# Seven products in place of eight for most of the first layer's input projection, with q, k, v and z parked in DRAM and the attention moved beside the conv output product

## The chip, the cores and the metric

The kernel runs on one core of one Trainium2 chip. The metric is device time in microseconds (us) of one execution; lower is better. TensorE (PE in the profile) does the matrix products, VectorE (DVE) and ScalarE (ACT) the element-wise work, GpSimd (POOL) some of it together with a DMA queue of its own, and SyncE (SP) issues most transfers.

## The reference

Two blocks follow each other on an activation of 1024 tokens by 1024 channels; the change lies in the first. All tensors are f32.

```python
h = rms_norm(x, norm_g)
u = h @ w_in        # v_c b_c c_c z_c q(1024) k(256) v(256) z_a gate_logits(2048)
y_c = b_c * causal_depthwise_conv(c_c * v_c, conv_w)
y_c = y_c * silu(z_c)
y_a = y_c @ w_conv_out
q = rms_norm(q per head, q_norm_g); k = rms_norm(k per head, k_norm_g)
o = sliding_window_attention(q, k, v, sinks) * silu(z_a)
y_b = o @ w_attn_out
gates = sigmoid(gate_logits + gate_b); g_a, g_b = split(gates, 2)
x = x + (g_a * y_a + g_b * y_b) @ w_out
```

The attention has 16 query heads and 4 key heads of 64 channels, blocks of 128 tokens and a window of 128. The second block (pooling and gated linear attention, cross attention, a feed-forward part) is not touched.

## The kernel before

**Layout.** Activations lie transposed, 128 channels by 512 tokens a tile; `kt` counts the eight channel tiles and `h` the two halves of the tokens. Every f32 operand is split into a high part and a low part (`S.copy` on ACT makes the high one, a subtraction on DVE the low one), and a product is three matmuls: high by high, high by low, low by high. A page is the weights for 128 output channels; it is loaded from DRAM on SP's queue into one of two raw buffers, cast on ACT (L282) and subtracted on DVE (L346).

**A dense step.** `dense(w, act, h)` is 24 matmuls of 512 columns into one PSUM bank. It calls `tick()` in its middle, and its caller calls `tick()` again behind it. A tick moves every generator in the list `side` one step on; that is how other work is set between matmuls. All engines take their instructions in the order in which the program writes them (`manual_schedule`).

**Seven products.** `wino` does two pages by two token halves as a 2 by 2 block product with seven half-size products in place of eight: 84 matmuls in place of 96. It needs sums of weight blocks (four additions on POOL for each page pair, L299 to L307, with their splits on ACT and DVE) and sums of activation blocks, T1 to T4, which the generator `sums` makes once for one norm (16 subtractions and 16 splits, started by `hT_sums`, which first reads the normalised activations back from DRAM). Each result is handed out in the middle of the sequence, through one of four callbacks: `c11` (as it lies in PSUM), `c22` and `c12` (a DVE addition or subtraction of a saved product makes them first) and `c21` (as it lies). Behind each callback stands a `tick()`.

```python
        prod(x, "A12", "B21", False)
        c11(x)
        tick()
        prod(y, "S3", "T3", False)
        c22(y, q5)
        tick()
```

**Order of the first block before the change.** k and v; z, eight pages, dense; q, eight pages, dense, each loaded twice because the order is by token half; the first four gate pages `gb`; the other gates and the attention output pages `ao`; the conv pages `cc`, `cv`, `cz`, `cb` for eight channel tiles, tile 0 dense and 1 to 7 by seven products; the gates `ga` by seven products; the conv output `co`, dense; then the output projection `wo`.

**The attention** is a generator of 32 units (two key pairs `p`, two halves `h`, four token blocks `b`, two head halves). Each step of it, one to a tick, takes the units through a pipeline: `scores` (PE, then DVE and ACT; for the first token block POOL first fills the tile, L892), `expo` (ACT), `finish` (POOL, L929), `turn` (PE transposes, then two POOL selections, L959), `differ` (POOL, L937 to L943, every second step) and `values` (PE, L972). It runs beside q and the first four gate pages. For each q tile, `stats` squares the tile on ACT (L846), sums over channels with eight small matmuls (L855) and takes a power on POOL (L859); `q_group` calls it one tick after the square is issued, in the middle of the next dense step.

Of the kernel before, what the change touches and what calls it, by code (L numbers as in the profile page):

```python
# [14 lines left out]
P = 128  # L15
# [63 lines left out]
def _stream():  # L79
    st = [("v", 0), ("v", 1)]  # L80
    st += [("z", p, j) for p in range(2) for j in range(4)]
    st += [("q", p, j) for p in range(2) for h in range(2) for j in range(4)]
    st += [("gb", m) for m in range(4)] + [("ao", m) for m in range(4)]
    for m in range(4, KT):
        st += [("gb", m), ("ao", m)]
    for c in range(KT):
        names = [("cc", c), ("cv", c), ("cz", c), ("cb", c)]
        st += names if c == 0 else [("pair", names[0], names[1]), ("pair", names[2], names[3])]
    st += [("pair", ("ga", m), ("ga", m + 1)) for m in range(0, KT, 2)]
    st += [("co", m) for m in range(KT)]  # L90
# [27 lines left out]
def _body(es, tc, nc, wp, vec, xT, memT, gk2, pw, cst, out, dbg):  # L118
# [39 lines left out]
    def dram(s):  # L158
        n = nm(s)
        return dpool.tile([P, HT], F32, name=n, tag=n)  # L160
# [546 lines left out]
    kp = [(pg("kh", F32R), pg("kl", F32R)) for _ in range(2)]  # L707
    wk = [[], []]
# [23 lines left out]
    def k_evac(o, p, h):  # L732
# [6 lines left out]
        def thread():  # L739
# [27 lines left out]
            V.tensor_tensor(kl[:, sl], kg, f(kh[:, sl]), ALU.subtract)  # L767

# [48 lines left out]


    oT = [[[None, None] for _ in range(4)] for _ in range(2)]

    def z_evac(p, j):
        def run(o, h):
            t = hp("o")
            S.activation(t, o, AF.Silu)
            oT[p][j][h] = t
        return run

    for p in range(2):
        for j in range(4):
            if (p, j) == (0, 0):  # L830
                first_two(("z", 0, 0), ("z", 0, 1), hT, z_evac(0, 0), z_evac(0, 1))
            elif (p, j) != (0, 1):
                both(("z", p, j), hT, z_evac(p, j))

    qT = {}
    rqt = {}

    def q_group(p, h):
        rq = spool.tile([P, 4, 4, 2], F32, name=nm("rq"), tag="rq", bufs=3)
        rqt[p, h] = rq  # L840
        for j in range(4):
            w = W.get(("q", p, j), pf=False)
            o = dense(w, hT, h, mid=W.pf)
            tick()
            sq = tp("qsq")
            S.activation(sq, o, AF.Square)  # L846
            qh, ql = hp("qh", F32R), hp("ql", F32R)
            S.activation(qh, o, AF.Copy, scale=col("q_norm_g"))
            V.scalar_tensor_tensor(ql, o, col("q_norm_g"), f(qh), ALU.mult, ALU.subtract)
            qT[p, j, h] = (qh, ql)  # L850

            def stats(sq=sq, j=j):
                st = ps("t", (P, 4, 64))
                for t in range(4):
                    T.matmul(st[:, t, :], sq[:, t * P:(t + 1) * P], blk2.rearrange("p a b -> p (a b)"), start=True, stop=True)  # L855
                ms = sm("ms", (P, 8))

                V.tensor_scalar(ms.rearrange("p (a b) -> p a b", b=2), st[:, :, 0:64:32], 1.0, 64 * EPS, ALU.mult, ALU.add)
                G.tensor_tensor(rq[:, :, j, :], ms.rearrange("p (a b) -> p a b", b=2),  # L859
                                mhalf.rearrange("p (a b) -> p a b", b=2), ALU.pow)  # L860
                return
                yield

            side.append(stats())
# [115 lines left out]
    def attention():  # L980
        units = [Unit(p, h, b, half) for p in range(2) for h in range(2) for b in range(4) for half in range(2)]
        n = len(units)
        todo = [(j, h) for j in range(4) for h in range(2)]
        dv = None
        yield
        for i in range(n + 3):
            if 0 <= i - 1 < n:
                units[i - 1].expo()
            if 0 <= i - 3 < n:
                units[i - 3].values(dv)  # L990
            if i % 2 == 0 and 0 <= i - 2 < n and units[i - 2].n:
# [7 lines left out]
            if i >= n - 6 and todo:  # L999
                j, h = todo.pop(0)  # L1000
                osp[j][h] = split(oT[0][j][h], "o")
            yield
        while todo:
            j, h = todo.pop(0)
            osp[j][h] = split(oT[0][j][h], "o")
        for h in range(2):
            for j in range(4):
                osp[4 + j][h] = split(oT[1][j][h], "o", tp if j == 3 else None)
                if j % 2:
                    yield  # L1010

    q_group(0, 0)
    side.append(attention())
    for p, h in ((0, 1), (1, 0), (1, 1)):
        q_group(p, h)
    mg = []

    def gb_evac(m, fn):
        t = pg("mg")
        mg.append(t)  # L1020

        def run(o, h):
            S.activation(t[:, h * HT:(h + 1) * HT], o, fn, bias=col("gate_b", 8 + m))
        return run

    for m in range(4):
        both(("gb", m), hT, gb_evac(m, AF.Identity if m < 3 else AF.Sigmoid))
    drain()
    for m in range(3):
        S.activation(mg[m], mg[m], AF.Sigmoid)  # L1030

    mgd = grid(KT)

    def ao_evac(m):
        def run(o, h):
            sl = slice(h * HT, (h + 1) * HT)
            V.tensor_tensor(mg[m][:, sl], mg[m][:, sl], o, ALU.mult)
            mgd[m][h] = dram("mgd")
            nc.sync.dma_start(mgd[m][h], mg[m][:, sl])
        return run  # L1040

    for m in range(4):
        both(("ao", m), osp, ao_evac(m))
    for m in range(4, KT):
        both(("gb", m), hT, gb_evac(m, AF.Sigmoid))
        both(("ao", m), osp, ao_evac(m))
    dump("mgb", mg[0])


    reopen("q1pool", 16)  # L1050
    XB = {}

    def hT_sums():
        t = {}
        order = [(kt, h) for k in range(4) for kt, h in ((k, 0), (k, 1), (k + 4, 1))] + [(k, 0) for k in range(4, 8)]

        def loads():
            for i, (kt, h) in enumerate(order):
                t[kt, h] = (hp if (kt < 4) == (h == 0) or kt == 7 else hq)("ht")
                nc.sync.dma_start(t[kt, h], hraw[kt, h])  # L1060
                if i in (3, 7, 9, 11, 13):
                    yield

        g = loads()
        for _ in range(3):
            next(g)
            yield
        side.append(g)
        yield from sums(t, XB, {"T1": hp, "T2": hp, "T3": hq, "T4": hq})

    yc, ycd = grid(KT), grid(KT)

    class Conv:


        def __init__(self, c):
            self.c, self.cs, self.accs, self.cv = c, [None, None], [None, None], [None, None]

        def cc(self, o, h):
            self.cs[h] = tp("cc")  # L1080
            S.copy(self.cs[h], o)

        def cv_tile(self, h):
            self.cv[h] = tp("cvp", shape=(P, HT + 2))
            if h == 0:
                G.memset(self.cv[h][:, 0:2], 0.0)
            return self.cv[h][:, 2:]

        def taps(self, h):
            w0, w1, w2 = (col("conv_w", k * 8 + self.c) for k in range(3))  # L1090
            cv = self.cv[h]
            if h:
                V.tensor_copy(cv[:, 0:2], self.cv[0][:, HT:HT + 2])
            acc = self.accs[h] = tp("yc")
            V.tensor_scalar(acc, cv[:, 0:HT], w0, None, ALU.mult)
            V.scalar_tensor_tensor(acc, cv[:, 1:HT + 1], w1, acc, ALU.mult, ALU.add)
            V.scalar_tensor_tensor(acc, cv[:, 2:HT + 2], w2, acc, ALU.mult, ALU.add)

        def cv_evac(self, o, h):
            V.tensor_tensor(self.cv_tile(h), o, self.cs[h], ALU.mult)  # L1100
            self.taps(h)

        def cz(self, o, h):
            t = tp("csz")
            S.activation(t, o, AF.Silu)
            V.tensor_tensor(self.accs[h], self.accs[h], t, ALU.mult)

        def cb(self, o, h):
            V.tensor_tensor(self.accs[h], self.accs[h], o, ALU.mult)
            ycd[self.c][h] = dram("ycd")  # L1110
            nc.sync.dma_start(ycd[self.c][h], self.accs[h])

        def first(self):
            def c22(y, q5):
                V.tensor_tensor(self.cv_tile(1), y, q5, ALU.add)

            def c12(z, q5):
                t = self.cs[1] = tp("cc")
# [3 lines left out]
            def c21(y):  # L1122
                self.cv_evac(y, 0)
                self.taps(1)
# [910 lines left out]
```

## Time and profile before

| | |
|---|---|
| Median of three runs | 2454.65 us (2453.22 to 2457.58) |
| The profiled execution's own time | 2452.95 us |
| Its span, from the first to the last instruction | 2451.2 us |
| PE busy | 2406.3 us, 98% |
| DVE, ACT, POOL busy | 1408.7, 964.5, 519.1 us |
| Mean granted TensorE clock | 0.996 |
| DMA | 223.00 MB, mean 91 GB/s |

A busy time adds up the instructions that overlap nothing; matmuls are pipelined, so that one of 512 columns is shown as 0.39 us long while the next one starts 0.23 us after it. Lengths of stretches are therefore taken from start to start.

### The profile page before, as it was taken

How to read it: one execution, taken by the hardware profiler on the slowest of the kernel's cores; microseconds unless marked ns; L12 is line 12 of the kernel's file. 1: busy time of each engine (PE TensorE's matmuls, PEld its weight loads, DVE VectorE, ACT ScalarE, POOL GpSimd, SP SyncE). 2: the span in 40 equal slices, each digit the busy share in tenths (PEclk: the TensorE clock that was granted, in tenths of full speed). 3: DMA queues.
4: the chain of work that ended last, by engine and by line, in shares of the span. 5: the costliest groups of instructions: out<-in, count | busy, mean ns of one | idle time of the engine just before them, and what ended most of it. 6: DMA issues, size and time to landing. Idle time of an engine off the chain costs nothing.

```text
span 2451.2 us, 30538 instructions
## 1 busy us (share of the span) xinstructions
PE 2406.3 (98%) x11694; PEld 1973.6 (81%) x11694; DVE 1408.7 (57%) x2223; ACT 964.5 (39%) x1784; POOL 519.1 (21%) x529
## 2 busy tenths in 40 slices
PE   8999999999999999999999999999999999999998
PEld 7887777888888888886888888888778887878887
DVE  6416676118666634555435556555678888874435
ACT  5326665113333242234322334444455555552212
POOL 3115653003333321021001110001223333310003
PEclk9999999999999999999999999999999999999999
DMA  4211111223222138231110245222422222244222
GB/s 156 92 53 52 35 40 41 84 85 122 69 73 74 61 109 304 87 97 51 35 36 29 79 128 180 95 82 95 155 78 82 78 78 78 78 150 158 90 80 91
DMA packets 86259, 223.00 MB, mean 91 GB/s; under 512 B 9792, under 2 KB 12256, under 8 KB 86112
## 3 DMA queue, kind: packets, MB, share of 16 engines
q1 hardware_dynamic: 82992, 212.65, 25.6%
q0 software_dynamic: 2576, 7.87, 0.9%
q8 instruction: 92, 1.51, 0.2%
q10 hardware_dynamic: 544, 0.52, 0.1%
q14 instruction: 55, 0.45, 0.1%
HBM read 180.11 MB, written 40.89 MB: 90 GB/s over the span
## 4 chain that ended last, share of the span: by engine, by line
PE 82%; DVE 8%; ACT 5%; POOL 2%; issue 2%; DMA 1%; SPq 0%; DVEq 0%; POOLq 0%; ACTq 0%
PE psmm L382 16%; PE psmm L384 16%; PE psmm L383 16%; PE pss L411 4%; PE pss L412 4%; PE pss L413 4%; PE psmm L412 3%; PE psmm L411 3%; PE psmm L413 3%; ACT pr L921 1%; PE pst L413 1%; PE pst L412 1%; PE pst L411 1%; PE pso L412 1%; PE pso L411 1%
## 5 line engine op out<-in xcount | busy, mean ns | idle before, releaser
L382 PE MATMUL psmm<-xnh,wh 128*128 128x512 f32 x832 | 332.8, 400 | 3.0 <-ACT wh L282 3.0
L384 PE MATMUL psmm<-xnh,wl 128*128 128x512 f32 x832 | 326.5, 392 | 2.6 <-DVE wl L346 2.6
L383 PE MATMUL psmm<-xnl,wh 128*128 128x512 f32 x832 | 325.6, 391 | 1.1 <-POOL u L1730 0.8
L346 DVE TENSOR_TENSOR wl<-wr,wh 128x1024 fp32r<-128x1024 f32 (+2 forms) x163 | 196.6, 1206 | 210.4 <-ACT wh L282 210.2
L282 ACT CAST wh<-wr 128x1024 fp32r<-128x1024 f32 (+2 forms) x163 | 165.1, 1013 | 272.7 <-PE psmm L383 264.3
L567 POOL TENSOR_TENSOR sq<-sq,sq 128x512 f32<-128x512 f32 (+1 forms) x58 | 70.6, 1217 | 643.8 <-ACT sq L563 642.8
L299 POOL TENSOR_TENSOR ws<-wr 128x512 f32<-128x512 f32 x37 | 57.8, 1563 | 634.1 <-DMA wr<-in_wp_dram 557.2
L382 PEld LDWEIGHTS psmm<-xnh,wh 128*128 128x128 f32 x832 | 157.0, 189 | 42.4 <-issue 5.8
L384 PEld LDWEIGHTS psmm<-xnh,wl 128*128 128x128 f32 x832 | 156.9, 189 | 38.0 <-DVE wl L346 4.3
L383 PEld LDWEIGHTS psmm<-xnl,wh 128*128 128x128 f32 x832 | 157.0, 189 | 33.6 <-POOL u L1730 1.2
L411 PE MATMUL pss<-T,wsh 128*128 128x512 f32 x444 | 176.9, 398 | 0.4
L413 PE MATMUL pss<-T,wsl 128*128 128x512 f32 x444 | 174.4, 393 | 0.0
L412 PE MATMUL pss<-T,wsh 128*128 128x512 f32 x444 | 174.4, 393 | 0.0
L331 DVE TENSOR_TENSOR wsl<-ws,wsh 128x512 fp32r<-128x512 f32 x148 | 145.3, 1024 | 18.2 <-ACT wsh L313 18.2
L384 PE MATMUL psmm<-fh,wl 128*128 128x512 f32 (+1 forms) x300 | 116.0, 387 | 1.0 <-DVE wl L346 1.0
L413 PE MATMUL psmm<-xnh,wl 128*128 128x512 f32 x296 | 115.4, 390 | 0.8 <-DVE wl L303 0.8
L382 PE MATMUL psmm<-fh,wh 128*128 128x512 f32 (+1 forms) x300 | 116.0, 387 | 0.0
L383 PE MATMUL psmm<-fl,wh 128*128 128x512 f32 (+1 forms) x300 | 115.9, 386 | 0.0
L412 PE MATMUL psmm<-xnl,wh 128*128 128x512 f32 x296 | 115.5, 390 | 0.0
L411 PE MATMUL psmm<-xnh,wh 128*128 128x512 f32 x296 | 115.4, 390 | 0.0
L563 ACT ACTIVATE sq<-x 128x512 f32<-128x512 f32 (+1 forms) x80 | 47.1, 588 | 165.3 <-DVE x L1250 110.0
L1741 DVE SCALAR_TENSOR_TENSOR fa<-u,vt,fa 128x512 f32<-128x512 f32 x88 | 79.2, 900 | 48.8 <-ACT fa L1740 45.1
(442 smaller groups left out, 5832.4 us busy)
## 6 DMA issues: line engine op xcount, KB each, us to landing
wr<-in_wp_dram SPq DMA_DIRECT2D x230, 512.0 KB, 3.5
act<-fa SPq DMA_DIRECT2D x44, 256.0 KB, 2.1
fr<-act SPq DMA_DIRECT2D x44, 256.0 KB, 4.6
wr<-in_wp_dram SPq DMA_DIRECT2D x24, 384.0 KB, 3.1
xd<-x SPq DMA_DIRECT2D x32, 256.0 KB, 4.4
x<-xd SPq DMA_DIRECT2D x32, 256.0 KB, 3.9
x<-in_xT_dram SPq DMA_DIRECT2D x16, 256.0 KB, 5.3
hraw<-xn SPq DMA_DIRECT2D x16, 256.0 KB, 2.0
```

What stands on the lines that cost most here:

```text
L282: S.copy(hi[:, :n], raw[:, :n])
L299: G.tensor_tensor(sg[0], a21, a22, ALU.add)
L331: V.tensor_tensor(lo, raw, f(hi), ALU.subtract)
L346: V.tensor_tensor(lo, raw, f(hi), ALU.subtract)
L382: T.matmul(out_ap, lh, rh, start=first, stop=False)
L383: T.matmul(out_ap, lh, rl, start=False, stop=False)
L384: T.matmul(out_ap, ll, rh, start=False, stop=last)
L411: T.matmul(o, lh, rh, start=first and kt == 0, stop=False, skip_group_check=True)
L412: T.matmul(o, lh, rl, start=False, stop=False, skip_group_check=True)
L413: T.matmul(o, ll, rh, start=False, stop=kt == 3, skip_group_check=True)
L567: eng.tensor_tensor(self.acc, self.acc, sq, ALU.add)
L1741: V.scalar_tensor_tensor(a, u[:, 1:HT + 1], w1, a, ALU.mult, ALU.add)
```

## The change

- z of `p` 1, all of q, all of `gb` and the conv tile 0 go by seven products, twelve page pairs more. `hT_sums` starts in the z stage, as soon as the second half of the norm is done and k and v are on their way to DRAM.
- k, v, q (both parts each), z and both gates are written to DRAM on SP's queue as they are made.
- The attention starts with `co`. `att_in` reads k, q, v and z back on POOL's queue: for both `p` of half 0 ahead of `co` (16 and 14 transfers of 256 KB), and for half 1 at the attention's steps 9 and 17 (16 and 14). Its units are ordered by half first.
- `co` and `ao` run by token half, so each of their pages is loaded and split twice; q's pages only once. The product of `co` with its gate goes to DRAM and comes back in `ao`, which now ends the stage.
- `stats` of q is put in `side` inside the callback, so it runs at the tick right behind it.

The core of the diff:

```diff
 def _stream():
     st = [("v", 0), ("v", 1)]
-    st += [("z", p, j) for p in range(2) for j in range(4)]
-    st += [("q", p, j) for p in range(2) for h in range(2) for j in range(4)]
-    st += [("gb", m) for m in range(4)] + [("ao", m) for m in range(4)]
...
+    st += [("z", 0, j) for j in range(4)]
+    st += [("pair", ("z", 1, j), ("z", 1, j + 1)) for j in (0, 2)]
+    st += [("pair", ("q", p, j), ("q", p, j + 1)) for p in range(2) for j in (0, 2)]
+    st += [("pair", ("gb", m), ("gb", m + 1)) for m in range(0, KT, 2)]
     for c in range(KT):
...
+        st += [("pair", ("cc", c), ("cv", c)), ("pair", ("cz", c), ("cb", c))]
     st += [("pair", ("ga", m), ("ga", m + 1)) for m in range(0, KT, 2)]
-    st += [("co", m) for m in range(KT)]
+    st += [("co", m) for m in range(KT)] * 2
+    st += [("ao", m) for m in range(KT)] * 2
...
+    def hT_sums():
+        while None in [x[1] for x in hT] or len(kd) < 8 or len(vd) < 4:
+            yield
+        reopen("q1pool", 16)
...
+    def q_out(p, j, h, o):
...
+        sq = tp("qsq")
+        S.activation(sq, o, AF.Square)
+        qh, ql = tp("qh", F32R), tp("ql", F32R)
+        S.activation(qh, o, AF.Copy, scale=col("q_norm_g"))
+        V.scalar_tensor_tensor(ql, o, col("q_norm_g"), f(qh), ALU.mult, ALU.subtract)
+        qd[p, j, h] = dram("qdh"), dram("qdl")
+
+        def stats():
+            for dst, src in zip(qd[p, j, h], (qh, ql)):
+                nc.sync.dma_start(dst, f(src))
+            st = ps("t", (P, 4, 64))
+            for t in range(4):
+                T.matmul(st[:, t, :], sq[:, t * P:(t + 1) * P], blk2.rearrange("p a b -> p (a b)"), start=True, stop=True)
...
+        side.append(stats())
...
+    def pair(na, nb, X, evac):
+
+        def c22(y, q5):
+            t = tp("c22")
+            V.tensor_tensor(t, y, q5, ALU.add)
+            evac(1, 1, t)
...
+        wino((na, nb), X, lambda x: evac(0, 0, x), c22, c12, lambda y: evac(1, 0, y))
...
+    while "T1" not in XB:
+        tick()
...
+    for j in (0, 2):
+        pair(("z", 1, j), ("z", 1, j + 1), XB, lambda i, h, o: z_out(1, j + i, h, o))
+    for p in range(2):
+        for j in (0, 2):
+            pair(("q", p, j), ("q", p, j + 1), XB, lambda i, h, o: q_out(p, j + i, h, o))
...
+    reopen("gpool2", 8)
...
+    def att_in(p, h):
+
+        if h == 0:
+            kp[p] = pg("kh", F32R), pg("kl", F32R)
+        for i in range(2):
+            nc.gpsimd.dma_start(f(kp[p][i][:, h * HT:(h + 1) * HT]), kd[p, h, i])
         for j in range(4):
...
+            qT[p, j, h] = hp("qh", F32R), hp("ql", F32R)
+            for i in range(2):
+                nc.gpsimd.dma_start(f(qT[p, j, h][i]), qd[p, j, h][i])
...
+        units = [Unit(p, h, b, half) for h in range(2) for p in range(2) for b in range(4) for half in range(2)]
...
+            if i in (9, 17):
+                att_in(i // 16, 1)
...
+    for p in range(2):
+        att_in(p, 0)
+    gate_in(gin, gad, 0, 0)
     while None in [yc[c][0] for c in range(KT)]:
         tick()
...
+    side.append(attention())
+    for h in range(2):
+        for m in range(KT):
+            w = W.get(("co", m))
+            gate_in(gin, gad, m + 1, h)
+            if h == 0 and m == 4:
+                side.append(reload([(ycd[c][1], yc[c], 1) for c in range(KT)], "yc", 2))
...
+            o = dense(w, yc, h)
+            t = gin[m, h]
+            V.tensor_tensor(t, t, o, ALU.mult)
+            mcd[m][h] = dram("mcd")
+            nc.sync.dma_start(mcd[m][h], t)
+            tick()
```

## Rows read from the trace of the kernel before

**Rows 1.** The page: busy time of each engine (share of the span) and its instructions.
```profile
PE 2406.3 (98%) x11694; PEld 1973.6 (81%) x11694; DVE 1408.7 (57%) x2223; ACT 964.5 (39%) x1784; POOL 519.1 (21%) x529
```

**Rows 2.** Timeline of PE, conv tile 0: start, us, instruction, count, idle before.
```profile
545.17 0.40 PE L382 MATMUL psmm<-xnh,wh 128*128 128x512 f32 x1
...
588.71 0.62 PE L445 MATMUL pss<-xnh 128*128 128x512 f32 x2
```

**Rows 3.** Timeline of PE, first matmuls of the second and the eighteenth seven-product pair.
```profile
609.47 0.39 PE L411 MATMUL psmm<-xnh,wh 128*128 128x512 f32 x1
...
918.22 0.39 PE L411 MATMUL psmm<-xnh,wh 128*128 128x512 f32 x1
```

**Rows 4.** Timeline of PE: first matmul of `values`, units 1, 22 and 28.
```profile
204.64 0.39 PE L972 MATMUL pso<-pch,vh 128*128 128x512 f32 x1
...
345.26 0.39 PE L972 MATMUL pso<-pch,vh 128*128 128x512 f32 x1
...
379.77 0.40 PE L972 MATMUL pso<-pch,vh 128*128 128x512 f32 x1
```

**Rows 5.** Timeline of PE: a group of `stats` between two matmuls of a dense step.
```profile
168.66 1.00 PE L855 MATMUL pst<-blk,qsq 128*128 128x64 f32 x8
169.47 0.48 PE L382 MATMUL psmm<-xnh,wh 128*128 128x512 f32 x1
```

**Rows 6.** POOL's power by line, and what L972 waited for.
```profile
L859 POOL TENSOR_TENSOR rq<-ms,mhalf x16: 1650/2553/2557, 169.9 to 346.1; 128x8 f32<-128x8 f32 x16
...
  POOL pph L959: 12.5, 21
```

**Rows 7.** Timeline, the kernel's end: addition, square, sum over channels [idle before <- releaser].
```profile
2441.01 0.42 DVE L1890 TENSOR_TENSOR x<-x,psmm 128x256 f32<-128x256 f32 x1 [1.02 <-PE psmm L384]
2441.53 0.42 ACT L563 ACTIVATE sq<-x 128x256 f32<-128x256 f32 x1 [1.08 <-DVE x L1890]
2442.00 0.55 PE L574 MATMUL pst<-mC,sq 128*128 128x64 f32 x3 [0.18 <-ACT sq L563]
```

**Rows 8.** Timeline, seven products: the last matmul of a product, its reader on ACT.
```profile
591.88 0.39 PE L413 MATMUL psmm<-xnh,wl 128*128 128x512 f32 x1
...
592.31 0.58 ACT L418 ACTIVATE pss<-psmm 128x512 f32<-128x512 f32 x1 [2.47 <-PE psmm L413]
```

**Rows 9.** By line, ns shortest/median/longest: square of q, addition as in `c22`, splits of T.
```profile
L846 ACT ACTIVATE qsq<-psmm x16: 597/610/622, 166.1 to 337.4; 128x512 f32<-128x512 f32 x16
...
L1772 DVE TENSOR_TENSOR u<-pss,q x19: 691/692/693, 1837.5 to 2189.5; 128x512 f32<-128x512 f32 x19
...
L462 DVE TENSOR_TENSOR T<-ht,T x16: 677/685/1781, 570.6 to 603.1; 128x512 fp32r<-128x512 f32 x16
```

**Rows 10.** Timeline of POOL as `co` begins: first and last transfers of 24.
```profile
936.52 0.54 POOL L1212 DMA_DIRECT2D mg<-mgd  x1 [18.81 <-PE pss L413]
...
950.21 3.17 POOL L645 DMA_DIRECT2D x<-in_xT_dram  x5 [0.20 <-issue]
```

**Rows 11.** Windows: busy of PE, PEld, DVE, ACT, POOL; clock, DMA share, GB/s.
```profile
936.50:954.00 17.50, 17.50 (x78) 14.45 (x77) 10.35 (x17) 6.86 (x13) 12.25 (x23) 1.00 0.96 350
...
339.00:414.00 75.00, 74.12 (x412) 59.11 (x411) 55.88 (x157) 49.06 (x150) 36.02 (x55) 1.00 0.09 29
```

**Rows 12.** By line, L904 on DVE: idle time until the fill on POOL (us, times).
```profile
  POOL pr L892: 5.8, 3
```

**Rows 13.** Timeline, attention beside `gb`: last selection of a pair, its reader on PE.
```profile
368.67 0.63 POOL L959 TENSOR_SCALAR_AFFINE_SELECT ppl<-pcl 128x512 fp32r<-128x512 f32 x1
...
380.47 0.39 PE L972 MATMUL pso<-pph,dvh 128*128 128x512 f32 x1
```

**Rows 14.** Windows round two pauses of PE, with the granted clock behind each.
```profile
20.90:25.40 4.50, 0.97 (x8) 0.77 (x8) 4.36 (x6) 3.28 (x6) 1.21 (x1) 1.00 0.61 243
25.50:28.90 3.40, 3.40 (x19) 3.40 (x18) 1.93 (x4) 0.00 (x0) 0.00 (x0) 0.50 0.02 5
76.00:87.00 11.00, 8.77 (x43) 7.14 (x42) 7.43 (x13) 7.03 (x10) 5.85 (x5) 1.00 0.40 143
```

More of the change, by code (lines that the diff above doesn't have):

```diff
@@ L835, in _body @@
[L835 to L840, printed above, removed]
-        for j in range(4):
[L842 to L864, printed above, removed]
@@ new lines, in v_out, with loads @@
+    def v_out():
+        yield
+        for h in range(2):
+            for i, t in enumerate(vv[h]):
+                vd[h, i] = dram("vd", (P, 4, 256))
+                nc.sync.dma_start(vd[h, i], f(t))
+    side.append(v_out())
+    XB = {}
+    def hT_sums():
+        while None in [x[1] for x in hT] or len(kd) < 8 or len(vd) < 4:
+            yield
+        reopen("q1pool", 16)
+        t = {}
+        order = [(kt, h) for k in range(4) for kt, h in ((k, 0), (k, 1), (k + 4, 1))] + [(k, 0) for k in range(4, 8)]
+        def loads():
+            for i, (kt, h) in enumerate(order):
+                t[kt, h] = (hp if (kt < 4) == (h == 0) or kt == 7 else hq)("ht")
+                nc.sync.dma_start(t[kt, h], hraw[kt, h])
+                if i in (3, 7, 9, 11, 13):
+                    yield
+        g = loads()
+        for _ in range(3):
+            next(g)
+            yield
+        side.append(g)
+        yield from sums(t, XB, {"T1": hp, "T2": hp, "T3": hq, "T4": hq})
@@ new lines, in _body @@
+    side.append(hT_sums())
+    first_two(("z", 0, 0), ("z", 0, 1), hT, *[lambda o, h, j=j: z_out(0, j, h, o) for j in range(2)])
+    for j in (2, 3):
+        both(("z", 0, j), hT, lambda o, h: z_out(0, j, h, o))
+    while "T1" not in XB:
+        tick()
+    XB["B11"], XB["B21"] = [hT[k][0] for k in range(4)], [hT[k + 4][0] for k in range(4)]
+    XB["B22"] = [hT[k + 4][1] for k in range(4)]
+    fill_banks(XB["B11"][0][0])
+    for j in (0, 2):
+        pair(("z", 1, j), ("z", 1, j + 1), XB, lambda i, h, o: z_out(1, j + i, h, o))
@@ new lines, in _body @@
+    for c in range(KT):
+        cv = Conv(c)
+        cv.first()
+        cv.second()
+    yc = grid(KT)
+    for m in range(0, KT, 2):
+        if m == KT - 2:
+            side.append(reload([(ycd[c][0], yc[c], 0) for c in range(KT)], "yc"))
+            next(side[-1])
+        pair(("ga", m), ("ga", m + 1), XB, lambda i, h, o: gate_out(gad, "gad", m + i, h, tp("ga"), o))
+    reopen("gpool2", 8)
+    kp, vv = [None, None], [None, None]
+    qT, oT = {}, [[[None, None] for _ in range(4)] for _ in range(2)]
@@ L980, in attention @@
     def attention():
-        units = [Unit(p, h, b, half) for p in range(2) for h in range(2) for b in range(4) for half in range(2)]
+        units = [Unit(p, h, b, half) for h in range(2) for p in range(2) for b in range(4) for half in range(2)]
         n = len(units)
-        todo = [(j, h) for j in range(4) for h in range(2)]
+        todo = []
         dv = None
-        yield
+        for _ in range(3):
+            yield
         for i in range(n + 3):
@@ L990, in attention @@
                 units[i - 3].values(dv)
+                if i % 8 == 2:
+                    u = units[i - 3]
+                    todo += [(u.p, j, u.h) for j in range(4)]
             if i % 2 == 0 and 0 <= i - 2 < n and units[i - 2].n:
@@ L998, in attention @@
                 units[i].scores()
-            if i >= n - 6 and todo:
-                j, h = todo.pop(0)
-                osp[j][h] = split(oT[0][j][h], "o")
+            if i in (9, 17):
+                att_in(i // 16, 1)
+            if todo:
+                p, j, h = todo.pop(0)
+                osp[4 * p + j][h] = split(oT[p][j][h], "o")
             yield
         while todo:
[L1004 to L1047, printed above, removed]
@@ L1050, in _body @@
[L1050 to L1066, printed above, removed]
-            yield
-        side.append(g)
-        yield from sums(t, XB, {"T1": hp, "T2": hp, "T3": hq, "T4": hq})
@@ L1147, in _body @@
-    side.append(hT_sums())
-    for c in range(KT):
-        cv = Conv(c)
-        if c == 0:
-            both(("cc", c), hT, cv.cc)
-            both(("cv", c), hT, cv.cv_evac)
-            both(("cz", c), hT, cv.cz)
-            both(("cb", c), hT, cv.cb)
-            while "T1" not in XB:
-                tick()
-            XB["B11"], XB["B21"] = [hT[k][0] for k in range(4)], [hT[k + 4][0] for k in range(4)]
-            XB["B22"] = [hT[k + 4][1] for k in range(4)]
-            fill_banks(XB["B11"][0][0])
-        else:
-            cv.first()
-            cv.second()
@@ L1237, in _body @@
-    side.append(mg_thread(1, KT))
-    dump("mg", mg[0])
+    side.append(attention())
+    for h in range(2):
+        for m in range(KT):
[3 more added lines that the diff above has]
+                side.append(reload([(ycd[c][1], yc[c], 1) for c in range(KT)], "yc", 2))
+            while None in [yc[c][h] for c in range(KT)]:
+                tick()
[4 more added lines that the diff above has]
+            nc.sync.dma_start(mcd[m][h], t)
+            tick()
@@ new lines, in _body, with ao_in @@
+    gbi = {}
+    def ao_in(m, h):
+        gate_in(gbi, gbd, m, h)
+        gate_in(cin, mcd, m, h)
+    xs = grid(KT)
+    ao_in(0, 0)
+    for h in range(2):
+        for m in range(KT):
+            w = W.get(("ao", m))
+            ao_in(m + 1, h)
+            if h and m >= 4:
+                for i in (0, 1):
+                    load_x(0, 2 * (m - 4) + i, nc.gpsimd)
+            while None in [osp[c][h] for c in range(KT)]:
+                tick()
+            o = dense(w, osp, h)
+            t = gbi[m, h]
+            V.tensor_tensor(t, t, o, ALU.mult)
+            V.tensor_tensor(t, t, cin[m, h], ALU.add)
+            mgs[m][h] = split(t, "mg")
+            tick()
@@ L1240, in residual @@
+    for kt in range(KT):
+        load_x(1, kt, nc.gpsimd)
     def residual(wname, act, gname, nxt, fast=True, norm=None, between=None, away=None, back=None):
```

237 lines of the change are left out of this document (104 added, 133 removed).

## The prediction

> **What bounds the kernel now.** I read the page's busy times first. TensorE is busy for 2406.3 of 2451.2 us, VectorE for 57%, ScalarE for 39%, POOL for 21% [rows 1]. So the time is the number of matmuls, at their pitch, plus the holes between them, and what another engine does counts only where a hole ends with it. Next I read TensorE's timeline from start to start, to price a page pair both ways. Dense, conv tile 0 takes 588.71 − 545.17 = 43.54 us for two pairs, 21.77 each; its 192 matmuls give a pitch of 0.227 us [rows 2]. By seven products, sixteen pairs take 918.22 − 609.47 = 308.75 us, 19.30 each [rows 3], with all the weight sums in them. Third came the attention, by the starts of `values`: units 22 to 28, beside `gb`, take (379.77 − 345.26) / 6 = 5.75 us each, while 21 units beside q take 345.26 − 204.64 = 140.62 [rows 4]. Last I looked at what ends TensorE's waits there, and at windows round a pause.
>
> **The change part by part.** The sum is made against the profiled execution, 2452.95 us (span 2451.2 and 1.75 round it); the median of the runs lies 1.7 above it.
>
> *Twelve pairs by seven products.* 12 × (21.77 − 19.30) = −29.7 us. The extra weight sums are in the 19.30. That z, q, k, v and gates go to DRAM is costed at nothing: SP issues it, and beside `gb` the DMA share is 0.09 [rows 11]. If that cover were gone, a write would delay a page load on the same queue.
>
> *Attention out of the q stage.* A `stats` group costs TensorE 169.47 − 168.66 = 0.81 us [rows 5]. Eleven lie in the 140.62 us, so 21 × 5.75 + 11 × 0.81 = 129.7 is explained and 10.9 is lost. What ended TensorE's waits at the values matmul was POOL's selection, 12.5 us in 21 waits, and in POOL's queue ahead of selections stand the 16 powers of 2.55 us [rows 6]. Beside `co` no power runs, so the gain lies between 0 and 10.9. But VectorE is busy for 55.88 of 75 us beside `gb` [rows 11], and gets the multiplication of `co` by its gate and a page per step. I take −9.
>
> *`stats` at the next tick.* TensorE now comes to the small matmuls at once and waits for the product's end, perhaps an addition, and the square. From the last matmul of a product to its reader is 592.31 − 591.88 = 0.43 us [rows 8]; the square takes 0.61, the addition 0.69 [rows 9]; from addition to square the gap is 0.10 (441.43 to 441.53), from square to the sum's matmul 0.05 [rows 7]. One pitch of 0.227 would have passed anyway. Direct results (c11, c21): 0.43 + 0.61 + 0.05 − 0.23 = 0.86. Those through the addition: 0.43 + 0.69 + 0.10 + 0.61 + 0.05 − 0.23 = 1.65. Eight of each: 20.1 us. That is the lower end. If the additions were stretched as far as the longest split is, from 0.69 to 1.78 beside POOL [rows 9], eight of them would make 29. I take 22. Queued behind the waiting matmuls is only the next product. The square stands in ScalarE's queue ahead of that result's two copies, and nobody waits for these soon.
>
> *T1 to T4.* They were begun 16 ticks ahead of the first seven-product pair. Now `hT_sums` waits for the last write of k and comes about 12 ahead. By the order of the program T2 is one tick late for its product and T3 two, so three steps run with no matmul beside them. A step is two or three VectorE operations of 0.69, 1.7 us on average: +5. Nothing if VectorE catches up during the products before; 10 if they are stretched toward 1.78 [rows 9].
>
> *The reload ahead of `co`.* Thirty transfers stand in POOL's queue ahead of the first fill of the attention. Now 23 transfers go out there: the first, at 936.52, had to wait for the end of the last `ga` pair (call that E, about 937.5), and the last are done at 953.38, 0.73 us each and 0.54 bare [rows 10], at a DMA share of 0.96 [rows 11]. Thirty by a mean of 0.65 end at E + 18.6, so the fill ends and its reader passes at about E + 19.6. `scores` comes at the fourth tick, E + 10.9, and the next unit's, at E + 13.6, needs the PSUM that the reader of the fill frees; that this reader waits for POOL already occurs, 5.8 us in 3 times [rows 12]. Late by 6; then comes `turn` of unit 0, whose chain starts only after the fill, for about 1.8 (an estimate from three operations of some 0.6). After 3.53 us without matmuls the clock was 0.50 for 3.4 us, 1.7 us lost [rows 14]. In all +9.5, taken as +9. At 0.73 per transfer it is 12; at nothing if the buffers of k come free early.
>
> *The reloads at steps 9 and 17.* Sixteen and fourteen transfers stand in POOL's queue amid the attention: 8.6 to 11.7 and 7.6 to 10.2 us. POOL's last selection of a pair ends at 369.30, and the next reader of the selections starts at 380.47 [rows 13]: 11.2 us, in which POOL is busy for 36.02 / 75 = 0.48 [rows 11], or 5.4, leaving 5.8. So it is late by 2.8 to 5.9 and 1.8 to 4.4, if all that work lies ahead of the reader, and by less if not. With VectorE's reload splits I take +5, between 0 and 10.
>
> *Costed at nothing:* q's pages once and `co`, `ao` pages twice (a page per dense step of 5.44 us; if the load or split were late, each step would show a wait for L282 or L346), and `ao` itself.
>
> Sum: −29.7 − 9 + 22 + 5 + 9 + 5 = +2.3. So 2455.25 on the profile's basis, and with its 1.7 below the median 2457.
>
> **Rivals.**
>
> *Faster: POOL gets its reloads through in time.* If the first k transfer is out some 9 us before E, the fill lies ahead of its `scores`, and if the mid reloads fit the free part of the turns, both terms vanish: −14, 2443 us. For it: bare issues take 0.54, and k's tiles lie in a region whose readers may be long done. Against: the first transfer had to wait for the last `ga` pair in the trace of before [rows 10]. It decides from a fill at E + 13.
>
> *Slower: the attention beside `co` is no smoother than beside q.* The gain of 9 turns to 0: 2466. For it: VectorE at 75% beside `gb`, before the added work [rows 11]. Against: the waits named POOL, not VectorE [rows 6].
>
> *Slower: the clock falls at the pauses of `stats`.* Eight longer pauses at 1.7 us each: +13.6, 2470.6. For it: the clock went to 0.50 (1.2 of 2.4 GHz) after 3.53 us of pause. Against: after 2.23 us it stayed at 1.00 [rows 14], and these are shorter. The Trainium skill, page "TensorE: Matmul & The Clock Gate", section "HAM oscillation — how this bites in real kernels", tells of a loop whose wait before every tile let the clock fall each time; by it this case would be the one above, and the two rows of the trace agree only in part.
>
> *Slower: each issue on POOL waits for VectorE.* If each of 60 issues stood behind one VectorE operation of 0.69 [rows 9], it would take 0.54 + 0.69 = 1.23: the first fill comes at E + 37, 17 later than above, and the mid reloads take 5 to 8 longer each: about +33, 2490 us. The trace speaks against it: 23 issues at 0.73 while VectorE was busy for 10.35 of 17.5 us [rows 10, 11]. The Trainium skill, page "SBUF — State Buffer", section "SBUF: two separate sides", names such a mechanism: transfers issued from GpSimd can't have their descriptors written while certain VectorE operations hold a port that both share. By that rule the sum would be 2490; the rows above don't show it.
>
> **How the numbers follow.** Runs of this kernel tell about 0.2%, 4.9 us, from no change: 2449.7 to 2459.6 counts as same. The forecast, 2457, gets 0.41 for that band; it is a sum of terms of opposite sign, each uncertain by some 5. POOL in time gets 0.25, and 0.02 goes to other ways to be faster: 0.27. Attention no smoother 0.14, clock 0.13, issues behind VectorE 0.05: slower 0.32. The range takes in the faster case and the two nearer slower ones, down by half the T term's 5 and to the clock's time: 2440 to 2470. Outside lie the last rival, half of the clock's and a few hundredths below.
>
> **What the profile after would show.** Pairs of z, `gb` and conv tile 0 at 19.3 us, q's at about 27.5 (four groups of 0.81 in each, with pauses of 0.86, 1.65, 1.65 and 0.86 ahead of them, ended by ACT's square). Two waits in the first z pair, ended by the T splits. A hole of some 6 us in `co`, 14 us after its start, ended by VectorE's masked copy behind POOL's fill, and the clock at 0.50 behind it. Waits of 1 to 6 us for selections after steps 9 and 17, ended by POOL. Between them, values of successive units 5.75 us apart. The prediction is wrong if `co` runs without the hole, if the pauses of `stats` are far from 1.25 on average, or if the attention's units come 6.2 us apart or more.

## The result, and the profile after

The changed kernel takes 2493.57 us (median of four runs, 2487.67 to 2500.05) against 2455.1: a ratio of 1.0157 (95% interval 1.0127 to 1.0186), 1.6% slower. It lies above the range of 2440 to 2470; 2457 was forecast. The profiled execution took 2496.53 us, 43.6 more than the one of before, where the sum had come to +2.3. So 41 us are to be found. Line numbers are those of the new kernel.

The page first, to be held against [rows 1]: TensorE is busy for 12 us less, and the span is 43.5 longer. The products were saved; holes and a lower clock ate them.

```profile
PE 2394.4 (96%) x11550; PEld 1959.4 (79%) x11550; DVE 1471.7 (59%) x2303; ACT 1010.2 (40%) x1871; POOL 608.5 (24%) x629
```

Then windows: the first and the second z pair, the four q pairs together, three stretches within the first q pair, and POOL's three blocks of transfers (columns as in [rows 11]).

```profile
122.19:155.24 33.05, 23.81 (x85) 18.32 (x84) 22.64 (x24) 11.48 (x20) 14.68 (x8) 0.85 0.20 71
155.24:174.47 19.23, 19.23 (x86) 15.77 (x84) 7.01 (x8) 7.75 (x13) 6.00 (x4) 1.00 0.31 110
174.47:297.21 122.74, 104.84 (x466) 83.12 (x464) 36.22 (x64) 40.49 (x68) 45.87 (x29) 0.92 0.28 103
182.90:188.50 5.60, 4.27 (x22) 3.07 (x20) 2.58 (x5) 2.20 (x4) 1.65 (x1) 1.00 0.29 108
188.50:195.50 7.00, 5.50 (x20) 4.24 (x20) 2.73 (x6) 1.24 (x2) 1.64 (x1) 0.76 0.19 75
195.50:202.00 6.50, 5.51 (x20) 4.27 (x20) 1.00 (x3) 1.25 (x3) 1.64 (x1) 0.74 0.23 83
757.70:786.30 28.60, 15.83 (x77) 12.50 (x76) 5.32 (x7) 5.94 (x7) 16.65 (x31) 0.85 0.97 367
841.00:853.60 12.60, 6.09 (x32) 3.97 (x31) 11.70 (x32) 7.75 (x25) 8.72 (x18) 0.82 0.84 303
890.00:910.00 20.00, 13.53 (x71) 10.03 (x70) 9.92 (x31) 8.29 (x29) 13.65 (x24) 0.84 0.66 236
```

An undisturbed pair takes 19.23 us, close to the 19.30 of [rows 3]. The first z pair takes 13.8 more. The q pairs take 122.74, where 4 × (19.23 + 4 × 0.81) = 89.9 would be without pauses: 32.8 more, of which about 0.08 × 122.74 = 9.8 is lowered clock (an estimate from the mean of the window). All three blocks of transfers have TensorE idle and the clock down.

TensorE's waits in the order of time, from its timeline (in brackets the idle time and who ended it); the last line is ScalarE's, just ahead of the last wait:

```profile
130.99 0.50 PE L411 MATMUL pss<-T,wsh 128*128 128x512 f32 x1 [3.20 <-DVE T L461]
141.34 0.51 PE L411 MATMUL pss<-T,wsh 128*128 128x512 f32 x1 [3.65 <-DVE T L461]
144.70 0.79 PE L411 MATMUL pss<-T,wsh 128*128 128x512 f32 x1 [2.39 <-DVE T L461]
...
183.98 1.10 PE L882 MATMUL pst<-blk,qsq 128*128 128x64 f32 x8 [0.74 <-ACT qsq L871]
189.40 1.11 PE L882 MATMUL pst<-blk,qsq 128*128 128x64 f32 x8 [1.50 <-ACT qsq L871]
196.39 1.26 PE L882 MATMUL pst<-blk,qsq 128*128 128x64 f32 x8 [1.49 <-ACT qsq L871]
...
786.83 0.81 PE L1073 MATMUL pss<-kh,qh 64*128 64x128 f32 x2 [13.30 <-DVE pr L1078]
...
854.64 1.12 PE L1123 MATMUL pst<-ident,pr 128*128 128x128 f32 x4 [6.98 <-POOL pr L1103]
...
907.05 0.79 PE L1146 MATMUL pso<-pch,vh 128*128 128x512 f32 x1 [6.47 <-ACT pch L1125]
906.21 0.30 ACT L1115 CAST dvh<-pwr 128x128 fp32r<-128x128 f32 x1 [8.42 <-POOL pwr L1113]
```

POOL's timeline shows what stood ahead: thirty transfers from the first line to the fill (L1066), the first again held until the last `ga` pair, and VectorE's masked copy behind the fill.

```profile
757.75 0.63 POOL L1027 DMA_DIRECT2D kh<-kd  x1 [39.33 <-PE pss L412]
758.44 0.54 POOL L1027 DMA_DIRECT2D kl<-kd  x1
...
779.70 0.54 POOL L1031 DMA_DIRECT2D ql<-qdl  x1 [0.67 <-DMA o<-zd]
780.64 0.54 POOL L1031 DMA_DIRECT2D qh<-qdh  x1 [0.40 <-DMA o<-zd]
...
784.70 1.06 POOL L1038 DMA_DIRECT2D o<-zd  x2 [0.37 <-issue]
785.76 0.54 POOL L1066 MEMSET pr<- 128x512 f32 x1
...
786.33 0.77 DVE L1078 COPY_PREDICATED pr<-iC,pss 128x256 f32<-128x256 uint8 x2 [14.57 <-POOL pr L1066]
```

Read it from the end back: `scores` of the second unit waits for the masked copy, that for the fill, the fill for thirty transfers. Each of these is 0.54 us long; the first eight go out back to back, and most of the later ones wait for an earlier transfer to land, 10.6 of the 28.0 us in all. `co` began at 758.66, so the fill came 27.1 us into it; the forecast had the last transfer at 18.6. By the list of the change all thirty are of 256 KB, but v's two are twice that:

```profile
vh<-vd POOLq DMA_DIRECT2D x2, 512.0 KB, 8.3
```

(Size and median time from issue to landing, from the list of transfers; `vl` has the same size.)

### The profile page after: what moved, and what is told of

Its sections match the earlier page's. It is cut to its first block, busy times and chain, and to the rows that moved or that the text cites. A ratio compares the mean times of both kernels' runs of the same rounds, so it can differ in the third digit from the quotient of the medians.

```text
span 2494.7 us, 30966 instructions
## 1 busy us (share of the span) xinstructions
PE 2394.4 (96%) x11550; PEld 1959.4 (79%) x11550; DVE 1471.7 (59%) x2303; ACT 1010.2 (40%) x1871; POOL 608.5 (24%) x629
## 3 DMA queue, kind: packets, MB, share of 16 engines
q8 instruction: 91, 1.49, 0.2%
## 5 line engine op out<-in xcount | busy, mean ns | idle before, releaser
L411 PE MATMUL pss<-T,wsh 128*128 128x512 f32 x588 | 232.4, 395 | 9.2 <-DVE T L461 9.2
L410 PE MATMUL pss<-T,wsh 128*128 128x512 f32 x588 | 236.6, 402 | 2.0 <-DVE cb L991 1.2
L345 DVE TENSOR_TENSOR wl<-wr,wh 128x1024 fp32r<-128x1024 f32 (+1 forms) x147 | 177.3, 1206 | 99.2 <-ACT wh L281 99.1
L412 PE MATMUL pss<-T,wsl 128*128 128x512 f32 x588 | 232.6, 396 | 0.0
L330 DVE TENSOR_TENSOR wsl<-ws,wsh 128x512 fp32r<-128x512 f32 x196 | 188.1, 1000 | 33.4 <-ACT wsh L312 32.4
L281 ACT CAST wh<-wr 128x1024 fp32r<-128x1024 f32 (+1 forms) x147 | 148.2, 1008 | 143.0 <-PE psmm L382 133.1
L381 PE MATMUL psmm<-xnh,wh 128*128 128x512 f32 x448 | 179.5, 401 | 3.0 <-ACT wh L281 3.0
L383 PE MATMUL psmm<-xnh,wl 128*128 128x512 f32 x448 | 176.0, 393 | 1.3 <-DVE wl L345 1.3
L382 PE MATMUL psmm<-xnl,wh 128*128 128x512 f32 x448 | 176.0, 393 | 1.1 <-POOL u L1735 0.8
L412 PE MATMUL psmm<-xnh,wl 128*128 128x512 f32 x392 | 154.0, 393 | 1.6 <-DVE wl L302 1.6
L410 PE MATMUL psmm<-xnh,wh 128*128 128x512 f32 x392 | 154.6, 394 | 0.0
L411 PE MATMUL psmm<-xnl,wh 128*128 128x512 f32 x392 | 153.4, 391 | 0.0
L411 PEld LDWEIGHTS pss<-T,wsh 128*128 128x128 f32 x588 | 112.2, 191 | 34.1 <-DVE T L461 10.5
L410 PEld LDWEIGHTS pss<-T,wsh 128*128 128x128 f32 x588 | 111.9, 190 | 32.0 <-ACT pss L417 5.1
L412 PEld LDWEIGHTS pss<-T,wsl 128*128 128x128 f32 x588 | 112.0, 191 | 25.8
L302 DVE TENSOR_TENSOR wl<-wr,wh 128x1024 fp32r<-128x1024 f32 x49 | 60.9, 1243 | 85.9 <-ACT wh L296 85.9
```

Of the source, the lines that this page charges most:

```text
L281: S.copy(hi[:, :n], raw[:, :n])
L302: V.tensor_tensor(l12, r1, f(h12), ALU.subtract)
L330: V.tensor_tensor(lo, raw, f(hi), ALU.subtract)
L345: V.tensor_tensor(lo, raw, f(hi), ALU.subtract)
L381: T.matmul(out_ap, lh, rh, start=first, stop=False)
L382: T.matmul(out_ap, lh, rl, start=False, stop=False)
```

## The experiments

Gains are differences of medians against the changed kernel run once more, 2494.20 us. Where a stage is given, it is read from the profiled executions; `co` to `wo` is the time from the first matmul of `co` to the first of `wo`.

> The changed kernel once more, beside the two others, with nothing edited. Its earlier median of 2493.6 stands on four runs from 2488 to 2500; by the sum of the three separate gains (72) against the joint one (61) it should lie lower, about 2486. Where the gains overlap for another reason, it stays at 2493.

2494.20 us (2489.08 to 2497.28), ratio 1.0161 (1.0142 to 1.0180). The high value stands; its first z pair took 26.79 us in this profile against 33.05 in the other, the q pairs 122.68 against 122.74. So the z term scatters. Over all the profiles that keep that stage, the other eight first z pairs lie between 26.8 and 28.9 us: the 33.05 is the exception.

The q pairs scatter too, although these two agree. In the five other runs that leave the q stage as it is, with the same sixteen pauses, the four pairs took 122.68, 121.06, 120.97, 117.88 and 116.35 us; the last of these (the transfers on SP's queue):

```profile
167.27:283.62 116.35, 98.46 (x466) 78.36 (x464) 35.70 (x63) 41.10 (x69) 44.05 (x27) 0.97 0.30 108
```

A pair takes 28.2 to 28.3 us, 29.7 to 29.9 or 31.4 to 31.5 there: the clock fell behind none, one or two of its two long pauses and cost 1.6 us each time, six times in each of the two profiles of the changed kernel and twice in the one above. Differences of a few us between medians carry this.

**The statistics one tick later.**

```diff
             for dst, src in zip(qd[p, j, h], (qh, ql)):
                 nc.sync.dma_start(dst, f(src))
+            yield
             st = ps("t", (P, 4, 64))
...
-            return
-            yield
```

> The small matmuls of the statistics of q run one tick later; their writes to DRAM are issued where they were. Theory (the pauses ahead of these matmuls, and the clock that falls behind them, are the whole excess of the q stage): the four q pairs fall from 122.7 us to about 90 (19.23 + 4 x 0.81 each), so -32 us, about 2461. Rival (the clock falls there for another reason): only the pauses go, 16 of them, 20.6 us in all: about 2473, with the granted clock still at 0.89 to 0.94 in that stretch. Second rival (the tiles live longer and a buffer is late): new waits in the q stage, less than 15 us won.

2460.03 us (ratio 1.0024, 1.0014 to 1.0034): 34 less. The four q pairs in one window, clock 1.00:

```profile
166.53:256.79 90.26, 90.26 (x458) 76.41 (x457) 37.88 (x61) 40.69 (x69) 40.10 (x26) 1.00 0.37 136
```

One of the sixteen groups now falls behind this window and costs 0.9 us there, so one tick of delay wins 31.6 of the 32.8, and no buffer came late for it.

**The pauses filled.** The share of the clock in this, by itself:

```diff
             st = ps("t", (P, 4, 64))
+            hi = XB["B11"][0][0]
+            for _ in range(13 if h else 6):
+                T.matmul(st.rearrange("p a b -> p (a b)"), hi[:, :P], hi[:, :256], start=True, stop=True)
             for t in range(4):
```

> As after, but TensorE does 6 (direct results) or 13 (results through an addition) matmuls of 256 columns, whose output is overwritten, while it would wait for the square: the pauses stay as long, and TensorE is busy in them. Theory (the pauses lower the clock): granted clock 1.00 in the q stage, the four q pairs at about 110.5 us in place of 122.7, so -12 us, about 2481. Rival (the clock is lowered by something else, such as the transfers): clock and time as in after, about 2494.

2484.65 us (ratio 1.0123, 1.0102 to 1.0144): 9.6 less.

```profile
166.39:279.61 113.22, 112.99 (x617) 96.40 (x616) 35.72 (x63) 41.12 (x69) 44.05 (x27) 1.00 0.31 112
```

The stage still waits for the squares, but with TensorE busy the clock stays at 1.00, and the stage loses 9.5 us of its 122.7, near the 9.8 estimated from the windows. The pauses themselves and what goes with them are the other 23.

**Half of the pauses.**

```diff
                 nc.sync.dma_start(dst, f(src))
+            if h:
+                yield
             st = ps("t", (P, 4, 64))
...
-            return
-            yield
```

> Only the statistics of results through an addition run one tick later; the eight of direct results stay at the next tick, with their pauses of 0.74 us. Theory (the clock falls where pauses of 1.5 us follow each other): clock 1.00 in the q stage, its four pairs at about 24.2 us each, some 26 us under after. Rival (any pause lowers it): clock at 0.9, pairs at 26 us.

2467.40 us (ratio 1.0049, 1.0034 to 1.0064): 27 less. The stage at clock 1.00, and its first pair's groups:

```profile
164.86:260.36 95.50, 92.52 (x466) 77.27 (x464) 36.62 (x62) 41.12 (x69) 41.49 (x26) 1.00 0.36 131
```

```profile
176.69 1.10 PE L884 MATMUL pst<-blk,qsq 128*128 128x64 f32 x8 [0.74 <-ACT qsq L871]
183.22 1.00 PE L884 MATMUL pst<-blk,qsq 128*128 128x64 f32 x8
186.87 2.01 PE L884 MATMUL pst<-blk,qsq 128*128 128x64 f32 x16
```

Only one pause a pair was left, not the two that were meant: the delayed group of c12 runs ahead of c21's and covers its wait. So this shows that pauses of 0.74 us, one in about 24 us, left the clock at 1.00; for two in each pair it shows nothing.

**The sums T with more time.** One z pair dense:

```diff
-    st += [("pair", ("z", 1, j), ("z", 1, j + 1)) for j in (0, 2)]
+    st += [("z", 1, 0), ("z", 1, 1), ("pair", ("z", 1, 2), ("z", 1, 3))]
...
+    for j in (0, 1):
+        both(("z", 1, j), hT, lambda o, h: z_out(1, j, h, o))
     while "T1" not in XB:
         tick()
...
-    for j in (0, 2):
+    for j in (2,):
         pair(("z", 1, j), ("z", 1, j + 1), XB, lambda i, h, o: z_out(1, j + i, h, o))
```

> The z pages 0 and 1 of the second half are dense again, ahead of the seven-product pairs; the sums T start where they did, so they have 8 more ticks. Theory (T2 to T4 come too late for the first pair, because they are begun too late): the first z pair falls from 33.05 to 19.3 us, and a dense pair costs 2.5 more than one by seven products: -11 us, about 2482. Rival (VectorE is simply too full there, weight sums and T together, with its operations stretched to 1.7 us): the wait moves into the dense steps or stays in the first pair, less than 4 us won.

2480.32 us (ratio 1.0103, 1.0088 to 1.0118): 14 less. The first z pair, a single window:

```profile
140.22:159.40 19.18, 19.18 (x86) 15.77 (x84) 9.75 (x10) 8.29 (x15) 7.78 (x6) 1.00 0.29 104
```

No wait is left there, and none came up in the dense steps. Against the repeat, with its pair of 26.79, the edit is worth 26.79 − 19.18 − 2.5 = 5 by the profile, and 7 against a pair of 28.9; the rest of the 14 is scatter, 1.7 us of it in the q pairs of this profile (120.97).

**The transfers spread.**

```diff
-    for p in range(2):
-        att_in(p, 0)
+    for _ in att_in(0, 0):
+        pass
...
+        rest = [(att_in(1, 0), 0), (att_in(0, 1), 9), (att_in(1, 1), 17)]
...
-            if i in (9, 17):
-                att_in(i // 16, 1)
+            for g, at in rest:
+                for _ in range(3 if i >= at else 0):
+                    next(g, None)
```

(`att_in` yields after each transfer.)

> Only the 16 transfers of the first head pair stand ahead of the attention; the other 44 are issued three per attention step, beginning at steps 0, 9 and 17. Theory (what is late is the other work in POOL's queue behind a block of transfers): the waits of 13.3, 7.0 and 6.5 us go, with the lowered clock behind them; about -30 us, 2464. Rival (the data themselves are late, at a DMA share of 0.97 and 0.93 us per transfer): the scores of the first unit or the values wait for q, k, v instead, about -10 us, 2484.

2467.99 us (ratio 1.0053, 1.0038 to 1.0068): 26 less. From the first matmul of `co` to the first of `wo` it is 290.8 us, against 312.0 and 313.3 in the two runs of the changed kernel. TensorE's first waits now:

```profile
767.07 0.66 PE L1077 MATMUL pss<-kh,qh 64*128 64x128 f32 x2 [0.82 <-DVE pr L1082]
768.29 0.33 PE L1077 MATMUL pss<-kh,qh 64*128 64x128 f32 x2 [0.35 <-DMA qh<-qdh]
769.78 0.33 PE L1077 MATMUL pss<-kh,ql 64*128 64x128 f32 x2 [1.05 <-DMA ql<-qdl]
```

The rival has 1.4 us of truth: the data of q are the next to be late. Behind step 9 three units come 7.0, 7.0 and 8.6 us apart, with waits of 0.93 for VectorE, which splits reloaded tiles of `yc` there; with a whole block that work fell into the hole (VectorE was busy for 11.70 of 12.60 us there).

**Only the start split**, the two later blocks whole (the edit above with 3, 16 and 16 per step):

> Only 16 of the 30 transfers stand ahead of the attention, 14 follow three per step; the blocks of 16 and 14 at steps 9 and 17 stay whole. Theory: the wait of 13.3 us at the start goes (its lowered clock too, some 17 us in all), the waits of 7.0 and 6.5 us stay. Rival (they have one cause, the load of the DMA engines, so a better start moves the later ones too): the later waits change by more than 3 us.

2476.94 us (ratio 1.0088, 1.0069 to 1.0106): 17 less. The later waits are 7.18 and 6.41 us, as before; each block has its own price. By stage the start is worth less than the 17 expected: `co` to `wo` takes 301.8 us, 11.5 less than the repeat's 313.3, and spreading the two later blocks as well wins 11.0 more (290.8).

**The fill on VectorE**, `V.memset(pr, -1e30)` in place of `G.memset`:

> The fill of the attention's first units (four times) is done by VectorE in place of POOL, so that it no longer stands behind the transfers. Theory (the transfers hold up POOL's queue as a whole, the fill is only the first that is late): the wait of 13.3 us moves one tick on, to the transposes of the first unit, whose multiplication on POOL still stands behind the last transfer; the end of the hole stays at 28 us after the start of co, 1 to 4 us are won, about 2491. Rival (the fill is what is late): the hole goes, -13 to -17 us, about 2478.

2482.61 us (ratio 1.0100, 1.0085 to 1.0115): 12 less, near the rival's figure, but not by its mechanism.

```profile
762.98 0.33 PE L1073 MATMUL pss<-kh,qh 64*128 64x128 f32 x2 [0.79 <-DMA qh<-qdh]
764.09 0.33 PE L1073 MATMUL pss<-kh,ql 64*128 64x128 f32 x2 [0.67 <-DMA ql<-qdl]
765.54 0.33 PE L1073 MATMUL pss<-kh,qh 64*128 64x128 f32 x2 [1.13 <-DMA qh<-qdh]
766.50 0.47 PE L1073 MATMUL pss<-kh,ql 64*128 64x128 f32 x2 [0.51 <-DMA ql<-qdl]
778.05 1.11 PE L1123 MATMUL pst<-ident,pr 128*128 128x128 f32 x4 [6.78 <-POOL pr L1103]
```

The wait moved on to the transposes, whose multiplication stands behind the last transfer, and the hole still ends 30.7 us after `co` began (747.33). By stage, `co` to `wo` takes 305.1 against 313.3, 8 us won, more than the 4 that I had allowed: about two dense half-steps more run before the hole, which begins 23.9 us after `co` in place of 14.9. By chance the q pairs of this profile are short too (117.88).

**The transfers on SP's queue**, `nc.sync.dma_start` in place of `nc.gpsimd.dma_start` in `att_in`:

> All transfers of the attention's reload are issued on SP's queue in place of POOL's, at the same places of the program. Theory (a block of transfers holds up whatever stands behind it in its queue, and loads the DMA engines for 12 to 28 us): the waits for POOL go, but the pages of co stand behind the blocks on SP's queue, and TensorE waits for ACT's and VectorE's split of a page, 8 to 15 us at the start of co and 2 to 6 at steps 9 and 17; between 2476 and 2494. Rival (only POOL's queue is the trouble): no hole over 2 us, as where the transfers are spread, about 2468.

2482.64 us (ratio 1.0103, 1.0086 to 1.0119): 12 less. One hole of 17.07 us at the start, past the 15 that I had allowed, and none at steps 9 and 17, where I had expected 2 to 6. `co` to `wo` takes 303.3 us, 10 less than in the repeat.

```profile
777.15 0.80 PE L383 MATMUL psmm<-ych,wl 128*128 128x512 f32 x1 [17.07 <-DVE wl L345]
769.79 0.32 SPq L1196 DMA_DIRECT2D g<-gad  x1
775.27 0.69 DVE L1214 TENSOR_TENSOR g<-g,psmm 128x512 f32<-128x512 f32 x1 [24.68 <-DMA g<-gad]
775.88 1.22 DVE L345 TENSOR_TENSOR wl<-wr,wh 128x1024 fp32r<-128x1024 f32 x1
```

The hole is where I expected it, but not by a late page. The page whose low part was missing had been cast on ScalarE at 753.02, so it was there. What stood behind the block on SP's queue was the first gate tile (L1196); VectorE's product with it waited 24.68 us, and the page's subtraction stood behind that product in VectorE's queue. The load of the page after it stood behind the block too, and went out at 770.52. At steps 9 and 17 the last transfer of the block is out at 840.2 and 889.6, and the next page's load follows only at 843.56 and 891.41, right behind the subtraction that frees its raw buffer: there the block was through before the page could be asked for.

**All three edits:**

> The three edits together: statistics one tick later, one z pair dense, transfers spread. Theory (three separate causes): the gains add up, -33.5 - 13.3 - 25.6 = -72 us against after, about 2421, that is 1.4% under before. Rival (the gains overlap, for instance because the clock falls in the same places anyway): 2430 to 2445.

2432.53 us (2431.07 to 2434.91), ratio to the kernel before 0.9900 (0.9884 to 0.9917): it beats both. 62 less than the changed kernel where the separate gains add to 34 + 14 + 26 = 74, so the time lies where the rival had it. By stage in the profiles the gains do add up, without overlap: q 90.3 for 122.7, −32.4; `co` to `wo` 290.7 for 313.3, −22.6; the z part −5; together −60. What the single runs had beyond that is put down to the scatter of the z pair and of the clock (the q pairs of the two runs that left them alone took 121.0 and 121.1, not 122.7); this was not shown item by item.

## Why the prediction was wrong

The saving came as forecast; the waits that the new order adds were priced too low. The two largest misses are the clock that falls behind the pauses of `stats` (11 us) and the blocks of transfers at steps 9 and 17 (13 us).

*Twelve pairs*: −29.7 forecast, 12 × (21.77 − 19.23) = −30.5 found. Right.

*Attention out of the q stage*: −9 forecast. First to last unit's `values` took 197.1 us before, 188.2 without its eleven groups of 0.81; after, 200.9. Three intervals at the holes, 14.98, 12.30 and the 7.60 that follows, in place of 5.68 each, add 17.8, which leaves 183.1:

```profile
846.12 0.47 PE L1146 MATMUL pso<-pch,vh 128*128 128x512 f32 x1 [0.21 <-DVE o L1150]
861.10 0.40 PE L1146 MATMUL pso<-pch,vh 128*128 128x512 f32 x1
...
894.75 0.39 PE L1146 MATMUL pso<-pch,vh 128*128 128x512 f32 x1
907.05 0.79 PE L1146 MATMUL pso<-pch,vh 128*128 128x512 f32 x1 [6.47 <-ACT pch L1125]
```

So −5 in place of −9; most units are 5.68 apart, and the last four, beside `ao`, 6.2 to 7.0.

*`stats` at the next tick*: 22 forecast, 32.8 found. The pauses were right: from the last matmul's start to the group's, less a pitch, 183.98 − 182.85 − 0.23 = 0.90 and 189.40 − 187.51 − 0.23 = 1.66, against 0.86 and 1.65; eight of each are 20.5. The step that failed is the clock's: "these are shorter" than a pause of 2.23 us that had left it at 1.00 [rows 14]. That row was one pause alone. Here pauses of 0.74, 1.50, 1.49 come within 13 us, and behind the second the granted clock was 0.76, then 0.74, with 0.50 (1.2 of 2.4 GHz) from 190.9 to 193.4. The rival "the clock falls at the pauses", which had 0.13, came true with 9.5 to 9.8 of its 13.6 us in the two profiles of the changed kernel; the filled pauses show it. It does not come true at every pause: with the same pauses other profiles lost as little as 3.1 (116.35 against the 113.22 of the filled pauses), and why the clock falls behind one pause and not behind the next stays open. The Trainium skill's section named there ("TensorE: Matmul & The Clock Gate", "HAM oscillation — how this bites in real kernels") tells of a loop whose wait before every tile lets the clock fall each time. The trace agrees in part: repeated pauses did lower it, but these are shorter than the waits told of there, and it fell behind some of them only.

*T1 to T4*: +5, with 10 as the upper bound. Found 13.8 in the profiled run, 7.6 in the repeat, and 7.6 to 9.6 in the seven other profiles that keep the stage. The mechanism was right: T begun too late, VectorE's operations stretched, up to 1.77 us in that pair. In the profiled run the waits of 3.20, 3.65 and 2.39 us make 9.2; in the repeat they make 4.9, the forecast's figure. Left out was the clock that falls with such waits, 0.85 over that pair in the profiled run: 4.6 us there, 2.7 in the repeat.

*The reload ahead of `co`*: +9, found about 14: a wait of 13.3 in place of 6, and some clock. The chain was right, to its place (the first transfer 0.9 us before `co`, the hole 14.9 after its start). Mis-sized was the time per transfer: (785.76 − 757.75) / 30 = 0.93 us, where 0.54 to 0.73 had been read from 23 transfers of 256 KB. The sum counted transfers where bytes count: with v's two of 512 KB it is 8.4 MB, moved beside other traffic by DMA engines that are 0.97 busy at 367 GB/s. The split start bears out the size: from the first matmul of `co` to the first of `values` it takes 26.4 us in place of 38.8, and has 2.2 us of waits of its own left.

*Steps 9 and 17*: +5, found 17.8. This is the largest miss in proportion, though spreading these blocks won back only 11.0 of it. I took the selections as what would be late first, with 11.2 us of slack [rows 13]. But the block stands ahead of `finish` (L1103) too, whose reader, the transposes, comes one tick later, 2.7 us; and at step 17 ahead of `differ` (L1113), whose cast on ScalarE (L1115) then holds up the cast of the transposes (L1125) behind it. The block delays the consumer with the least slack, not the one that waited before.

The misses add to 4 + 11 + 9 + 5 + 13 − 1 = 41 of the 41 us. Each is read to about 1 us, so that they meet the 41 exactly is chance.

The rival of issues that wait for VectorE had forecast 2490 and is nevertheless refuted: single issues are 0.54 us long with VectorE busy for 11.70 of 12.60 us in the second block, and the waits between them end, nearly all, with a transfer's landing. The Trainium skill's rule of "SBUF: two separate sides" ("SBUF — State Buffer") is not what set the time here. The rival "POOL in time" needed the fill at E + 13, E being the end of the last `ga` pair; it came 27.1 us into `co`.

For "same" each added wait had to stay within its bounds. Three of the four went past the upper one in both profiles of the changed kernel, T1 to T4 in one of them, each time by a second effect that had no term of its own: the clock behind a wait, the load of the DMA engines, the queue of the next engine. None of the three signs named for a wrong prediction came: the hole was there, the pauses were 1.28 us on average, the units mostly 5.68 apart. They tested whether the mechanisms were there, and not what each would cost.

## What to carry to other kernels

Price a block of transfers by the work behind it whose consumer has the least slack, in the block's own queue and in the queues of the engines that wait for it, and by the bytes over the bandwidth, not by the issue time; then spread it. Where matmuls follow their producer's result, give them one tick: repeated small pauses cost their own length, and in clock up to half as much again (3 to 9.5 us beside 20.5 us of pauses here). A saved product is worth its time only after the holes have been looked for that its new order makes; here about 24 of 33 us (28 from eleven pairs, 5 from the attention's place) came through once three orders were mended (1.0% faster than before in place of 1.6% slower).

## What the runs showed of the hardware that was not expected

Pauses of TensorE of 0.74 to 1.50 us that follow each other lowered the granted clock to an average of 0.92 over 123 us, although one of 2.23 us had not; a pause of 0.74 in each pair alone did not either (1.00 over 95.5 us). The same pauses lowered it to 0.97 only in another run (over 116 us): it fell behind two to six of the eight long ones, for 1.6 us each time. A block of thirty transfers, 8.4 MB, held POOL's queue for 28.0 us, 10.6 of them in waits for earlier transfers to land. VectorE's subtractions for T, 128 by 512, mostly 0.68 us long, took up to 1.78 now and then, as they had before [rows 9].
